# Windowed attention on one core: loading the first query block as float32 over SyncE and casting it on GpSimd

## The chip, the cores and the metric

The kernel runs on one core of one Trainium2 chip. The metric is the device time of one launch, in microseconds (us). Before the change it was 943.04 us in the median of three runs (942.97 to 943.06). On one core a single run has no second core to be compared with, so "fast" here only means that no run lay over 1.5% above the fastest of its kernel; none did.

Five engines work side by side: TensorE (PE, its weight loads PEld), VectorE (DVE), ScalarE (ACT), GpSimd (POOL) and SyncE (SP). Sixteen DMA engines move the data between HBM and the core's SBUF.

## The reference, cut to what matters

```python
B, S, D, W = 4, 4096, 1536, 64                   # float32 q, k, v
logits = einsum('bnwd,bnud->bnwu', q_w, k_w) * D ** -0.5   # windows of 64 rows
attn   = softmax(logits)
out    = einsum('bnwu,bnud->bnwd', attn, v_w)
```

Each window of 64 rows attends to itself alone. So q, k and v are each read once and the result is written once: 302 MB in and 101 MB out, with little arithmetic on each byte.

## The kernel before

A unit is 512 rows (4 slots of 128 rows), and there are 32 units. For each, q, k and v are loaded by GpSimd's transfers, which cast float32 to float16 on the way, into one of two landing buffers each. GpSimd copies a landed block to the working buffer (`q16`, `k16`, `v16`) and at once requests the block of two units later:

```python
def hand_over(x, u, dst, m, g):
    gp.wait_ge(landed[x][u % NL], 16 * (...))   # the load has landed
    gp.wait_ge(m, u)                            # the unit before is done with the working buffer
    gp.tensor_copy(out=dst..., in_=landing[x][u % NL]...).then_inc(c_l, 1)
    ...
    gp.sem_inc(g, 1)                            # TensorE may use it
    request(x, u + NL)                          # the load of two units later

for u in range(1, N):
    hand_over("q", u, q16, m_q, g_q)
    hand_over("k", u, k16, m_k, g_k)
    gp.wait_ge(m_q, u + 1)
    store(u - 1)                                # behind it in program order: the next v
    hand_over("v", u, v16, m_v, g_v)
```

TensorE transposes q and k, multiplies them, and later multiplies the weights by v. VectorE and ScalarE empty its accumulators.

The first unit has no landing buffer: its blocks go straight into the working buffers. Its first slot of q came over SyncE as float32 into an output buffer, and GpSimd cast it; the other three slots came by GpSimd's casting transfer:

```python
first = rows(qf, 0, SLOTS, SLOTS)
nc.sync.dma_start(out=outs[0][:, 0, :], in_=first[:, 0, :D]).then_inc(d_r0, 16)
nc.gpsimd.dma_start(out=q16[:, 1:, :]..., in_=first[:, 0, D:]).then_inc(d_q0, 16)
load("k", 0, k16, d_k0)
...
load("v", 0, v16, d_v0)
for u in (1, 2):
    for x in "qkv":
        request(x, u)
nc.gpsimd.wait_ge(d_r0, 16)
nc.gpsimd.tensor_copy(out=q16[:, 0, :], in_=outs[0][:, 0, :]).then_inc(c_q, 1)
...
sy.wait_ge(c_q, 1)                       # SyncE releases TensorE
sy.sem_inc(g_q, 1)._wait_ge(d_q0, 16)
```

The softmax here doesn't subtract the row's maximum and nothing guards it: scores larger than these inputs give would overflow.

## Time and profile before

| | before |
|---|---|
| time, median | 943.04 us |
| span in the profile | 940.6 us |
| busiest engine | TensorE, 70% |
| DMA engines | full in all 40 slices |
| first transpose | 12.86 us |
| one load (3.146 MB read) or one store (3.146 MB) | 7.3 us |

How to read this: the row that is full names the bound, and the time of one transfer is then the ruler.

### The profile page before, as it was taken

The numbers are of one execution on the slowest core, as the hardware profiler recorded it, in microseconds if no ns is written. First come the engines' busy times: TensorE is split into PE (matmuls) and PEld (weight loads), VectorE is DVE, ScalarE is ACT, GpSimd is POOL, SyncE is SP. The second block draws the span as 40 slices with busy tenths as digits, with TensorE's granted clock in tenths as the row PEclk, the third lists the DMA queues.
The fourth block names the chain that finished last, engine by engine and source line by source line (L and its number), as shares of the span: only waits on it lengthen the run. The fifth ranks groups of instructions, "written<-read, shape, count | busy, mean of one in ns | idle before, by whom it ended". The sixth has DMA issues, their size and how long they took to land. (4 is left out here: it accounts for less than half of the span.)

```text
span 940.6 us, 11416 instructions
## 1 busy us (share of the span) xinstructions
PE 660.8 (70%) x4096; PEld 399.9 (43%) x3456; DVE 280.0 (30%) x453; ACT 335.8 (36%) x642; POOL 337.3 (36%) x226
## 2 busy tenths in 40 slices
PE   3787677766867767767677676776867768667673
PEld 2454345533444434454444443344434355334440
DVE  1333321333313323223332233322333223332232
ACT  1444432333333333332343324333333333343332
POOL 3344333344333443333423334233343333433221
PEclk9999987888888888887887978888888887898886
DMA  9999999999999999999999999999999999999998
GB/s 206 218 217 275 257 245 280 282 282 265 236 281 282 282 273 234 275 282 282 279 234 270 282 282 281 239 262 281 283 282 246 255 281 283 281 255 246 282 299 368
DMA packets 26796, 252.17 MB, mean 268 GB/s; under 512 B 2080, under 2 KB 2080, under 8 KB 10400
## 3 DMA queue, kind: packets, MB, share of 16 engines
q0 software_dynamic: 26352, 248.13, 100.7%
q1 hardware_dynamic: 432, 3.93, 1.1%
q14 instruction: 10, 0.08, 0.0%
q8 instruction: 2, 0.03, 0.0%
HBM read 301.99 MB, written 100.66 MB: 428 GB/s over the span
## 5 line engine op out<-in xcount | busy, mean ns | idle before, releaser
L155 PE MATMUL lt<-xq,xk 128*128 128x256 f16 x1536 | 217.2, 294 | 0.0
L143 PE MATMUL tp<-ident,k 128*128 128x128 f32 x768 | 150.7, 342 | 89.5 <-PEq L209 81.2
L292 POOL COPY v<-vl 128x3072 f32<-128x3072 f32 x31 | 85.0, 2742 | 294.6 <-DMA vl<-in_v_dram 294.6
L155 PEld LDWEIGHTS lt<-xq,xk 128*128 128x128 f16 x1536 | 160.5, 105 | 33.6
L143 PEld LDWEIGHTS tp<-ident,k 128*128 128x128 f32 x768 | 116.8, 178 | 109.7 <-issue 107.0
L143 PE MATMUL tp<-ident,q 128*128 128x128 f32 x768 | 112.6, 294 | 65.4 <-DVE xq L218 34.6
L218 ACT COPY xk<-tp 128x512 f32<-128x512 f32 x96 | 59.4, 618 | 271.7 <-ACTq L209 271.7
L184 PEld LDWEIGHTS <-et 128*128 128x128 f16 x384 | 34.6, 108 | 278.4 <-issue 272.7
L218 DVE COPY xk<-tp 128x512 f32<-128x512 f32 x96 | 66.5, 692 | 237.6 <-DVEq L209 237.6
L143 PEld LDWEIGHTS tp<-ident,q 128*128 128x128 f32 x768 | 91.3, 151 | 106.3 <-issue 105.6
L292 POOL COPY q<-ql 128x3072 f32<-128x3072 f32 x31 | 85.0, 2742 | 123.6 <-DMA ql<-in_q_dram 123.6
L292 POOL COPY k<-kl 128x3072 f32<-128x3072 f32 x31 | 85.2, 2747 | 108.8 <-DMA kl<-in_k_dram 108.8
L111 PE MATMUL o<-v,et 128*128 128x512 f16 x384 | 113.1, 439 | 0.0
L260 ACT ACTIVATE et<-lt,zeros 32x128 f16<-32x128 f32 x256 | 92.0, 360 | 39.4 <-ACTq L209 36.1
L111 PE MATMUL sp<-ones,et 128*128 128x1 f16 x256 | 25.7, 169 | 113.1 <-PEq L209 110.8
L218 ACT COPY xq<-tp 128x512 f32<-128x512 f32 x96 | 59.8, 623 | 119.4 <-ACTq L209 119.4
L247 DVE TENSOR_SCALAR out<-o,rs 128x512 f32<-128x512 f32 x128 | 91.1, 747 | 32.6 <-DVEq L209 28.3
L271 ACT ACTIVATE out<-tp,rs 128x512 f32<-128x512 f32 x64 | 44.0, 687 | 136.7 <-ACTq L209 107.9
L218 DVE COPY xq<-tp 128x512 f32<-128x512 f32 x96 | 66.3, 690 | 86.6 <-DVEq L209 86.2
L111 PE MATMUL tp<-v,et 128*128 128x512 f16 x256 | 91.9, 446 | 0.0
L237 DVE RECIPROCAL rs<-sp 128x2 f32<-128x2 f32 x64 | 10.7, 167 | 261.6 <-DVEq L209 261.5
L111 PE MATMUL lt<-v,et 128*128 128x512 f16 x128 | 57.9, 452 | 0.0
(22 smaller groups left out, 221.2 us busy)
## 6 DMA issues: line engine op xcount, KB each, us to landing
out_dram<-out POOLq DMA_DIRECT2D x31, 3072.0 KB, 61.7
ql<-in_q_dram POOLq DMA_DIRECT2D x31, 1536.0 KB, 54.9
kl<-in_k_dram POOLq DMA_DIRECT2D x31, 1536.0 KB, 54.9
vl<-in_v_dram POOLq DMA_DIRECT2D x31, 1536.0 KB, 54.9
out_dram<-out SPq DMA_DIRECT2D x2, 1536.0 KB, 8.4
k<-in_k_dram POOLq DMA_DIRECT2D x1, 1536.0 KB, 17.7
v<-in_v_dram POOLq DMA_DIRECT2D x1, 1536.0 KB, 24.1
q<-in_q_dram POOLq DMA_DIRECT2D x1, 1152.0 KB, 11.1
```

The costliest lines, as they stand in the source:

```text
L111: return nc.tensor.add_instruction(mybir.InstMatmult(name=nc.get_next_instruction_name(), engine=PE, ins=[low(rhs), low(w)], outs=[low(o)] ...
L143: ins = nc.tensor.transpose(tps[g % 2][:, r, j, :], pairs[:, c * P : (c + 1) * P], ident[:, :])
L155: ins = nc.tensor.matmul(lts[h][:, r, :, :], lhsT=halves(xk, c)[:, r, h, :, w], rhs=halves(xq, c)[:, :, h, :, w], start=(c == 0 and w == 0 ...
L184: ld = nc.tensor.ldweights(w)
L218: copy(out=dst, in_=tps[g % 2][:, :, :, :]).then_inc(f_c[g % 4], 1)
L237: ve.reciprocal(out=rs[:, n : n + R], in_=sp[:, n : n + R]).then_inc(n_d, 1)
L247: ins = ve.tensor_scalar_mul(scaled(u, n, j), bank(n, j), scalar1=rs[:, n : n + 1])
L260: ins = sc.activation(ets[h][s, :, :, s], lts[h][s, :, :, s], EXP, bias=zeros[s, 0:1], scale=scale)
L271: ins = sc.activation(scaled(u, n, j), bank(n, j), COPY, bias=0.0, scale=rs[:, n : n + 1])
L292: gp.tensor_copy(out=dst[:, :, :].bitcast(FP32), in_=landing[x][u % NL][:, :, :].bitcast(FP32)).then_inc(c_l, 1)
```

## The change

Its intent is a plainer start. The first q comes whole, as float32, over SyncE in one transfer, so GpSimd has one issue less. GpSimd casts it in one instruction, which stands behind its eight load issues.

```diff
-        first = rows(qf, 0, SLOTS, SLOTS)
-        nc.sync.dma_start(out=outs[0][:, 0, :], in_=first[:, 0, :D]).then_inc(d_r0, 16)
-        nc.gpsimd.dma_start(
-            out=q16[:, 1:, :].rearrange("p r d -> p (r d)"), in_=first[:, 0, D:]
+        nc.sync.dma_start(
+            out=slots(outs[0], 0, SLOTS, SLOTS), in_=rows(qf, 0, SLOTS, SLOTS)
         ).then_inc(d_q0, 16)
         load("k", 0, k16, d_k0)
 ...
-        nc.gpsimd.wait_ge(d_r0, 16)
-        nc.gpsimd.tensor_copy(out=q16[:, 0, :], in_=outs[0][:, 0, :]).then_inc(c_q, 1)
+        nc.gpsimd.wait_ge(d_q0, 16)
+        nc.gpsimd.tensor_copy(out=q16[:, :, :], in_=outs[0][:, :, :]).then_inc(c_q, 1)
 ...
         sy.wait_ge(c_q, 1)
-        sy.sem_inc(g_q, 1)._wait_ge(d_q0, 16)
+        sy.sem_inc(g_q, 1)
```

More of the change, by code (lines that the diff above doesn't have):

```diff
@@ L72 @@
     sp = ps("sp", [P, 4])
-    d_r0, d_q0, d_k0, d_v0 = (sem(n) for n in ("d_r0", "d_q0", "d_k0", "d_v0"))
+    d_q0, d_k0, d_v0 = (sem(n) for n in ("d_q0", "d_k0", "d_v0"))
     landed = {x: [sem(f"d_{x}{i + 1}") for i in range(NL)] for x in "qkv"}
```

## The prediction

> **What bounds the kernel now.** I read the page first, for the span, the busy shares and the DMA row.
>
> ```profile
> span 940.6 us, 11416 instructions
> ...
> PE 660.8 (70%) x4096; PEld 399.9 (43%) x3456; DVE 280.0 (30%) x453; ACT 335.8 (36%) x642; POOL 337.3 (36%) x226
> ...
> DMA  9999999999999999999999999999999999999998
> ...
> HBM read 301.99 MB, written 100.66 MB: 428 GB/s over the span
> ```
>
> No engine is busy more than 70%, while the 16 DMA engines are full in all 40 slices. So the transfers bound the kernel, and the test of any change is whether it adds bytes, adds transfer time, or lets the transfer queue run empty.
>
> Next, the start in the timeline, of which I show the GpSimd (POOL) steps and the first TensorE step.
>
> ```profile
> 0.95 0.38 SPq L303 DMA_DIRECT2D out<-in_q_dram  x1
> ...
> 1.48 0.68 POOL L304 DMA_DIRECT2D q<-in_q_dram  x1 [1.04 <-SPq L300]
> ...
> 7.30 1.51 POOL L319 CAST q<-out 128x1536 f16<-128x1536 f32 x1
> 12.86 1.57 PEld L143 LDWEIGHTS tp<-ident,q 128*128 128x128 f32 x8 [12.86 <-issue]
> ...
> 34.47 2.75 POOL L292 COPY q<-ql 128x3072 f32<-128x3072 f32 x1 [25.66 <-DMA ql<-in_q_dram]
> ...
> 41.74 2.75 POOL L292 COPY k<-kl 128x3072 f32<-128x3072 f32 x1 [3.40 <-DMA kl<-in_k_dram]
> ...
> 45.59 0.72 POOL L277 DMA_DIRECT2D out_dram<-out  x1
> ...
> 49.05 2.74 POOL L292 COPY v<-vl 128x3072 f32<-128x3072 f32 x1 [2.75 <-DMA vl<-in_v_dram]
> ```
>
> Each of these copies starts when its load lands, 7.3 us after the one before, not when the unit before it has finished. One load reads 3.146 MB from HBM; 3.146 MB in 7.25 us is 434 GB/s. The other landings fit the same ruler, from the list of DMA issues (last number: microseconds from issue to landing):
>
> ```profile
> out_dram<-out POOLq DMA_DIRECT2D x31, 3072.0 KB, 61.7
> ql<-in_q_dram POOLq DMA_DIRECT2D x31, 1536.0 KB, 54.9
> ...
> k<-in_k_dram POOLq DMA_DIRECT2D x1, 1536.0 KB, 17.7
> v<-in_v_dram POOLq DMA_DIRECT2D x1, 1536.0 KB, 24.1
> q<-in_q_dram POOLq DMA_DIRECT2D x1, 1152.0 KB, 11.1
> ```
>
> Added to their issue times: the rest of q0 (the first q) lands at 12.6, k0 at 2.16 + 17.7 = 19.9, v0 at 3.03 + 24.1 = 27.1. A steady load lands some 55 us after its issue, so seven transfers of 7.3 us stand in the queue: it does not live from hand to mouth. From k0's landing at 19.9 to the last v's copy at 917.4 there are 1 + 93 loads and 29 stores: 897.5 / 123 = 7.30 us each, and three more stores (21.9 us) give 939.3, next to the span of 940.6. That is the whole span, explained by transfers alone.
>
> **What the Trainium skill says.** "DMA: Bandwidth & Descriptors", Anatomy of one DMA, gives some 2 us fixed plus bytes over 436 GB/s; the trace agrees (434 GB/s, and slot 0 of q0, 0.79 MB, took 6.3 us beside other traffic). The same page, Issuing engines are not separate DMA queues, says that transfers from SyncE and GpSimd run on the same 16 engines and interleave, and its section Queues, rings and completion order says that an engine takes its queues in turn. The window table agrees as far as it goes: between 3 and 5 us, with both queues open, it shows 403 and 321 GB/s of written bytes, between the 217 of casting loads alone and the 434 of an uncast one. "GPSIMD Engine Reference", Engine selection, calls one-input elementwise work there about line rate; the trace has 1.51 us for 1536 columns, 0.98 ns each.
>
> **The change, part by part.**
>
> *Bytes.* HBM bytes stay: q0 is 3.146 MB read, as before. Only what is written into SBUF grows: three slots of float32 for float16, from 1.18 to 2.36 MB. Loads that write half (217 GB/s written, 434 read) and stores that write all (3.146 MB) both take 7.3 us, so a transfer costs by its larger side, and this growth should cost nothing: q0 stays a 7.25 us job.
>
> *Issues.* One GpSimd issue of 0.68 us goes; the eight left come 0.7 us earlier. The SyncE transfer still goes out at 0.95 us, so the engines start moving at the same time (in windows of 1 us, the DMA share is 0.17 in the second and 0.75 in the third microsecond).
>
> *Landing of q0.* Alone, from about 2.2 us: 7.25 of transfer and 2 of completion make 11.4. Sharing evenly with k0 all along, 2.2 + 14.5 + 2 = 18.7. SyncE's queue has a start of about 1.5 us before GpSimd's first bytes, so I estimate 17.5 us, and k0 no later than its 19.9, since both together are the same two jobs.
>
> *Cast.* 6144 columns for 1536: 4 x 1.51 = 6.0 us, all of it now on the path to the first transpose; before, the small cast ended at 8.8 while the other slots landed at 12.6. The first transpose starts at 17.5 + 6.0 + 0.3 (the gap from landing to TensorE before: 12.6 to 12.9) = 23.8 us instead of 12.9: **11 us later**.
>
> *What of it survives.* Unit 0 waited for k0 before (transposes of q ended at 18.8, those of k began at 20.16); that 1.4 us goes, so k's transposes begin at 29.7 instead of 20.16, 9.5 us later. Now each thing that unit 0 releases, against the landing that it has to beat:
> - q16 free (last copy of q, 19.6 before): about 30 after. q1 lands at 34.5. Hidden.
> - k16 free (last copy of k begins at 28.3 before): about 38. k1 lands at 41.7. Hidden, 4 us to spare.
> - v16 free (end of unit 0's outputs, 37.8 before): about 47.5. v1 lands at 49.05. Hidden by 1.5 us, or late by one or two.
> - The first store (45.59 before) waits on GpSimd for unit 1's last q copy, which follows unit 0's last product: about 52. The v1 copy stands behind it in program order, and begins at about 53 instead of 49; its new load goes out at about 56 instead of 52.4.
>
> So GpSimd slips by some 6 us and then 4. At 52 us the queue still holds q2, k2, v2, q3 and k3, which land from 56.4 to 86.1: more than 30 us of work. The order in the queue is program order and does not change, so a store or load put in 6 us late starts where it would have. TensorE's unit needs about 23 us when nothing is late (37.5 to 60 or so for unit 1), a unit's transfers 3 x 7.3 us until the first store gets its turn and 4 x 7.3 = 29.2 after that. So the lag shrinks from unit 2 on, and v3, which lands at 100.7 after store 0, should find GpSimd waiting. Nothing of the 11 us reaches the end. The sum: 943.0 + 0 (path) + 0 (bytes) + some tenths either way from how the two queues mix in the first 17 us.
>
> **The rivals.**
>
> *The late start goes through.* If units ran back to back, the end would move by the full 9 to 11 us: about 953, still only 1.1% slower. Against it: GpSimd's waits in the first 120 us are all for landings, and TensorE has 30% idle to catch up with. I give it 4%.
>
> *The queue runs dry for a moment.* GpSimd being late by 6 us with stores and loads costs if the queue were shorter than that. It would give 944 to 949. Against it: some 55 us from issue to landing. Some 5%.
>
> *The bytes written count.* If a float32 write cost beyond the read, 1.18 MB / 434 GB/s = 2.7 us: 945.7. The stores, at the same 7.3 us, speak against it. Some 8%.
>
> *A gain at the start.* From 5 to 10 us the page's windows show 205 GB/s written where steady loads show 217: about 5% lost in 5 us while small and large transfers from two queues mix. One large uncast transfer may move better: up to 1 us faster, 942. Some 15%.
>
> **Range and chances.** Most weight is on no change, within what the three runs before show (942.97 to 943.06) and a spread of a few tenths of a per cent for another run: 943.2 us, 8 in 10 from 941.5 to 945.3. None of the rivals reaches 2% (18.9 us) either way; what is left there is something unseen, such as a transfer from SyncE that holds up GpSimd's queue. Faster 0.01, within 2% 0.97, slower 0.02.
>
> **What would show it.** Right: the q0 landing 14 to 19 us; one cast of 5.9 to 6.2 us; first transpose between 20 and 26; k0, v0 and q1 landing within 1 us of 19.9, 27.1 and 34.5; the first store issued at about 52; GpSimd waiting for DMA again from unit 3 on, with the v3 copy within 1 us of 100.7; the DMA row full throughout; the last v copy within 2 us of 917.4. Wrong: landings from k1 on shifted by the same amount right to the end (the bytes or the mixing count), a DMA slice below 9 between 60 and 120 us (the queue ran dry), or v copies that wait for their buffer and not for DMA past unit 4 (TensorE does not catch up).

## The result, and the profile after

The changed kernel took 942.58 us in the median of six runs (942.19 to 943.18), the kernel before 942.93 us (942.65 to 943.06) over its six. The ratio is 0.9997 with a 95% interval of 0.9984 to 1.001: the same time. Ratios here are the mean time of one kernel's fast runs over that of the other's of the same rounds, so not quite the ratio of the medians quoted.

The page of the changed kernel, in the lines that answer to those shown of before:

```profile
span 940.6 us, 11415 instructions
...
PE 656.9 (70%) x4096; PEld 397.2 (42%) x3456; DVE 279.9 (30%) x453; ACT 335.6 (36%) x642; POOL 341.0 (36%) x225
...
DMA  9999999999999999999999999999999999999998
...
HBM read 301.99 MB, written 100.66 MB: 428 GB/s over the span
```

Same span, same bytes of HBM, same full DMA row. The start itself has changed a good deal. The timeline of the changed kernel (start, duration, engine, line; in brackets the idle time before and what ended it):

```profile
0.96 0.38 SPq L302 DMA_DIRECT2D out<-in_q_dram  x1
...
17.80 5.30 POOL L317 CAST q<-out 128x6144 f16<-128x6144 f32 x1 [10.99 <-DMA out<-in_q_dram]
23.47 1.57 PEld L143 LDWEIGHTS tp<-ident,q 128*128 128x128 f32 x8 [23.47 <-issue]
...
34.17 2.75 POOL L292 COPY q<-ql 128x3072 f32<-128x3072 f32 x1 [11.07 <-DMA ql<-in_q_dram]
...
41.42 2.75 POOL L292 COPY k<-kl 128x3072 f32<-128x3072 f32 x1 [3.37 <-DMA kl<-in_k_dram]
...
50.01 0.72 POOL L277 DMA_DIRECT2D out_dram<-out  x1 [4.73 <-ACTq L216]
...
50.73 2.76 POOL L292 COPY v<-vl 128x3072 f32<-128x3072 f32 x1
```

The first transpose comes 10.6 us later (23.47 against 12.86). Yet q1 and k1 are copied when they land, 0.3 us earlier than before. Of these steps only the first store (50.01 against 45.59) and the first v copy (50.73 against 49.05) are late, and they no longer wait for a transfer. What becomes of that lateness is in GpSimd's timeline of the changed kernel, two units on:

```profile
90.83 0.71 POOL L277 DMA_DIRECT2D out_dram<-out  x1 [0.73 <-ACTq L216]
100.77 2.74 POOL L292 COPY v<-vl 128x3072 f32<-128x3072 f32 x1 [9.22 <-DMA vl<-in_v_dram]
...
119.62 0.71 POOL L277 DMA_DIRECT2D out_dram<-out  x1
```

The third store waits 0.73 us for ScalarE, the fourth not at all, and the v copy at 100.77 waits 9.22 us for its landing. In the kernel before, the same copy stands at 100.72. The lag is gone after three units, and the last v copy starts at 917.38 in both kernels.

The list of transfers of the changed kernel (KB written, us from issue to landing):

```profile
ql<-in_q_dram POOLq DMA_DIRECT2D x31, 1536.0 KB, 54.9
...
out<-in_q_dram SPq DMA_DIRECT2D x1, 3072.0 KB, 16.8
...
k<-in_k_dram POOLq DMA_DIRECT2D x1, 1536.0 KB, 18.0
```

The first q lands at 0.96 + 16.8 = 17.8 us, and k0, issued at 1.48, at 19.5. The two share the engines and land almost together. A steady load still lands 54.9 us after its issue: the queue is as deep as before.

### The profile page after: what moved, and what is told of

Same layout as the page of the kernel before. It is cut to its first block, busy times and chain, and to the rows that moved or that the text cites. A ratio compares the mean times of both kernels' runs of the same rounds, so it can differ in the third digit from the quotient of the medians.

```text
span 940.6 us, 11415 instructions
## 1 busy us (share of the span) xinstructions
PE 656.9 (70%) x4096; PEld 397.2 (42%) x3456; DVE 279.9 (30%) x453; ACT 335.6 (36%) x642; POOL 341.0 (36%) x225
## 5 line engine op out<-in xcount | busy, mean ns | idle before, releaser
L143 PE MATMUL tp<-ident,k 128*128 128x128 f32 x768 | 146.9, 335 | 82.9 <-PEq L209 71.7
L143 PEld LDWEIGHTS tp<-ident,k 128*128 128x128 f32 x768 | 113.9, 174 | 102.8 <-issue 100.2
L237 DVE RECIPROCAL rs<-sp 128x2 f32<-128x2 f32 x64 | 10.7, 168 | 259.5 <-DVEq L209 259.3
## 6 DMA issues: line engine op xcount, KB each, us to landing
ql<-in_q_dram POOLq DMA_DIRECT2D x31, 1536.0 KB, 54.9
kl<-in_k_dram POOLq DMA_DIRECT2D x31, 1536.0 KB, 54.9
vl<-in_v_dram POOLq DMA_DIRECT2D x31, 1536.0 KB, 54.9
out<-in_q_dram SPq DMA_DIRECT2D x1, 3072.0 KB, 16.8
```

The lines of the kernel that those rows point to most:

```text
L143: ins = nc.tensor.transpose(tps[g % 2][:, r, j, :], pairs[:, c * P : (c + 1) * P], ident[:, :])
L237: ve.reciprocal(out=rs[:, n : n + R], in_=sp[:, n : n + R]).then_inc(n_d, 1)
```

## The experiments

My theory: the transfers bound the kernel, and the nine transfers put out at the start let compute begin late at no cost as long as that queue does not run dry. The rival: compute's start counts in full or in part. A second question is whether float32 in place of float16 in SBUF costs transfer time, and a third what a standstill of the engines costs. Every edit below is to the changed kernel, whose 942.58 us is the base; each run was timed in three rounds beside the kernel before (942.8 to 943.1 us), and all gave correct results.

### e1: the cast shared by three engines

```diff
-        nc.gpsimd.tensor_copy(out=q16[:, :, :], in_=outs[0][:, :, :]).then_inc(c_q, 1)
+        nc.gpsimd.tensor_copy(out=q16[:, 0, :], in_=outs[0][:, 0, :]).then_inc(c_q, 1)
+        nc.vector.wait_ge(d_q0, 16)
+        nc.vector.tensor_copy(out=q16[:, 1:3, :], in_=outs[0][:, 1:3, :]).then_inc(c_q, 1)
+        nc.scalar.wait_ge(d_q0, 16)
+        nc.scalar.copy(out=q16[:, 3, :], in_=outs[0][:, 3, :]).then_inc(c_q, 1)
 ...
-        sy.wait_ge(c_q, 1)
+        sy.wait_ge(c_q, 3)
```

> The cast is shared out: VectorE two slots, ScalarE one, GpSimd one, all behind the same landing at 17.8 us. First transpose at about 20.5 us instead of 23.5. My theory (transfers bound the kernel, the start of compute is hidden by the queue): 942.6 us, within 1 us of the changed kernel. Rival (the start of compute counts): 939.5 us, 3 us faster.

Measured: 942.61 us (942.33 to 942.97), with the first transpose at 20.86. Compute starts 2.6 us earlier and the time stays. The theory holds, and the cast is not worth speeding up here.

### e2, e3, e4: the cast seven, nine and thirteen times

```diff
-        nc.gpsimd.tensor_copy(out=q16[:, :, :], in_=outs[0][:, :, :]).then_inc(c_q, 1)
+        for i in range(7):          # 9 and 13 in e3 and e4
+            nc.gpsimd.tensor_copy(out=q16[:, :, :], in_=outs[0][:, :, :]).then_inc(c_q, 1)
+            nc.gpsimd.wait_ge(c_q, i + 1)
 ...
-        sy.wait_ge(c_q, 1)
+        sy.wait_ge(c_q, 7)          # 9 and 13
```

> The cast of 5.3 us runs seven times instead of once, one after the other: 6 x 5.3 = 31.8 us more before the first transpose, which comes at about 55.3 us. My theory: the nine transfers issued up front keep the DMA engines busy until v2 has landed at 70.7 us; the first of the next issues (q3) would follow unit 0's last q copy at 62, so at about 65.5 us, just in time. 943 us, at most 946. Rival (a late start goes through to the end): 942.6 + 31.8 = 974 us.

> The cast runs nine times: 8 x 5.3 = 42.4 us more, first transpose at about 66 us. My theory: q3 is issued at about 76 us, but the engines run out at about 69 us; the queue is dry for 9 us or so, and for one or two more around the first store: 954 us (950 to 958), and the DMA row of the profile shows a slice well below 9. Rival (goes through): 985 us. Rival (hidden without limit): 942.6 us.

> The cast runs thirteen times: 12 x 5.3 = 63.6 us more. My theory: beyond the point where the queue runs dry each further microsecond counts in full, so this is e3_cast_x9 plus 4 x 5.3 = 21.2 us, about 975 us. Rival (goes through from the first microsecond): 1006 us. A slope well below 1 between e3 and e4 would say that the queue refills and hides part of it again.

| | first transpose | time, median |
|---|---|---|
| e1 | 20.9 us | 942.61 us |
| changed kernel | 23.5 us | 942.58 us |
| e2 | 55.5 us | 944.78 us |
| e3 | 66.4 us | 956.24 us |
| e4 | 87.5 us | 976.98 us |

This is a flat line with a knee. The first 32 us of delay (23.5 to 55.5) cost 2.2 us; from e3 to e4, 21.1 us of delay cost 20.7 us. The knee lies where the queue runs dry. The page's DMA row of e3:

```profile
DMA  9987999999999999999999999999999999999997
```

And windows of 2 us of e3 around that place (busy time of PE, PEld, DVE, ACT and POOL with the number of instructions, then clock, DMA share and GB/s written):

```profile
66.00:68.00 2.00, 1.60 (x8) 1.57 (x8) 0.36 (x1) 0.00 (x0) 0.01 (x1) 1.00 1.02 212
68.00:70.00 2.00, 1.87 (x10) 1.51 (x8) 0.62 (x2) 0.63 (x1) 0.00 (x0) 1.00 0.31 61
70.00:72.00 2.00, 1.79 (x10) 1.12 (x9) 0.80 (x2) 0.62 (x1) 0.00 (x0) 1.00 0.00 0
...
76.00:78.00 2.00, 2.00 (x21) 1.77 (x19) 0.49 (x1) 0.62 (x1) 0.08 (x1) 1.00 0.73 98
...
92.00:94.00 2.00, 1.36 (x11) 0.88 (x9) 1.08 (x2) 0.66 (x1) 1.30 (x2) 1.00 0.43 98
```

The engines stop between 68 and 70 us, where the nine transfers end, and start again after q3's issue at 75.53; a second, shorter dip follows at the first store (issued at 92.70), as expected. The expected issue times (76 us for q3 in e3, 65.5 in e2) were right within 0.5 us, and the knee lies where they put it: e2's q3 is just in time, e3's is not.

e2 lies inside its expected range but 2.2 us above the changed kernel. This lateness is there in full at the v copy of unit 6 (2.2 us) and stays to the last (2.3), so it is not the slow loss described under e7. Its DMA share falls to 0.88 in the 2 us behind the first store's issue at 82.01 and to 0.69 from 112 to 114 us; but the changed kernel, too, has a 0.83 at its first store (82 to 84 us). What the 2.2 us are made of stays open.

### e5, e6: one more transfer, as float32 or with the cast in it

```diff
+        # e5: SyncE, behind its first transfer
+        nc.sync.dma_start(out=slots(outs[1], 0, SLOTS, SLOTS),
+                          in_=rows(qf, UR, SLOTS, SLOTS)).then_inc(d_x0, 16)
+        # e6 instead: GpSimd, behind v0
+        nc.gpsimd.dma_start(out=outs[1][:, 0:2, :]....bitcast(FP16),
+                            in_=rows(qf, UR, SLOTS, SLOTS)[:, 0, :]).then_inc(d_x0, 16)
+        # both: waited for before v0 is released to TensorE
+        sy.wait_ge(d_x0, 16)
```

> SyncE loads a second float32 block of 3.146 MB (the rows of q1, into an output buffer that unit 1 overwrites) right after the first; it holds up only the release of v0 to TensorE. My theory (a transfer costs by its larger side, and its time adds to the end): 942.6 + 7.25 = 949.9 us. Rival (what comes early lies in the head beside compute that has not begun, so it is hidden): 942.6 us.

> As e5, but GpSimd issues the extra load with the cast in the transfer: 3.146 MB read, 1.573 MB written, behind v0 in its queue. My theory (reads set the time of a load): the same 7.25 us more, 949.9 us, within 0.5 us of e5. Rival (bytes written into SBUF count): half, 946.2 us. That also prices the growth from float16 to float32 in the change: 0 against about 2.7 us.

Measured: e5 950.15 us (949.86 to 950.5), e6 949.95 us (949.74 to 950.16). So 7.6 and 7.4 us more than the changed kernel, and within 0.2 us of each other. The landing of q1, from GpSimd's timeline of e5:

```profile
41.42 2.75 POOL L292 COPY q<-ql 128x3072 f32<-128x3072 f32 x1 [18.39 <-DMA ql<-in_q_dram]
```

and of e6:

```profile
41.48 2.75 POOL L292 COPY q<-ql 128x3072 f32<-128x3072 f32 x1 [18.32 <-DMA ql<-in_q_dram]
```

Against 34.17 that is 7.25 and 7.31 us, whether 3.146 or 1.573 MB were written (the two also differ in the queue, SyncE's or GpSimd's). Both read the same, so between these two loads the bytes written made no difference. And the time counts although the compute engines have hardly begun: 7.3 us more of transfers in the head cost 7.4 to 7.6 us at the end, while 32 us more of cast in the same head cost 2.2.

### e7: GpSimd waits for the first q before its first issue

```diff
+        nc.gpsimd.wait_ge(d_q0, 16)
         load("k", 0, k16, d_k0)
 ...
-        nc.gpsimd.wait_ge(d_q0, 16)
         nc.gpsimd.tensor_copy(out=q16[:, :, :], in_=outs[0][:, :, :]).then_inc(c_q, 1)
```

> GpSimd waits for q0 before its first load issue instead of behind the eighth. The first q has all 16 engines to itself and lands at about 11.5 us instead of 17.8; eight issues of 5.3 us and the cast of 5.3 us then put the first transpose near 22 us, almost where it is in the changed kernel. My theory: what counts is the time in which the engines stand still between q0's last byte and k0's first, 2 to 3.5 us: 944.6 to 946 us. Rival (the start of TensorE is what counts): 941 to 942.6 us.

Measured: 948.45 us (947.67 to 949.16), 5.9 us more, with the first transpose at 23.59, 0.1 us from where it is in the changed kernel. So the same start of compute gives another time, and a time in the direction of the standing engines, but more than I had expected. The windows of 1 us of e7, same columns as above:

```profile
10.00:11.00 1.00, 0.00 (x0) 0.00 (x0) 0.00 (x0) 0.00 (x0) 0.00 (x0) 1.00 0.19 57
11.00:12.00 1.00, 0.00 (x0) 0.00 (x0) 0.00 (x0) 0.00 (x0) 0.00 (x0) 1.00 0.00 0
12.00:13.00 1.00, 0.00 (x0) 0.00 (x0) 0.00 (x0) 0.00 (x0) 0.45 (x1) 1.00 0.00 0
13.00:14.00 1.00, 0.00 (x0) 0.00 (x0) 0.00 (x0) 0.00 (x0) 0.91 (x3) 1.00 0.33 37
```

From the shares, the standstill is 0.81 + 1 + 1 + 0.67 = 3.5 us, and q1's copy starts at 37.66 against 34.17, also 3.5. The last v copy starts at 924.02 against 917.38: 6.6 us. So about half of this delay is the standstill, at the upper end of what I expected, and the other half comes afterwards, in small steps of the landings between units 3 and 20, with the DMA row full (more on it under e10). The theory is right in kind, and it left out this second part.

### e8: the first q by GpSimd's casting transfer like all others

```diff
-        nc.sync.dma_start(
-            out=slots(outs[0], 0, SLOTS, SLOTS), in_=rows(qf, 0, SLOTS, SLOTS)
-        ).then_inc(d_q0, 16)
+        load("q", 0, q16, d_q0)
         load("k", 0, k16, d_k0)
 ...
-        nc.gpsimd.wait_ge(d_q0, 16)
-        nc.gpsimd.tensor_copy(out=q16[:, :, :], in_=outs[0][:, :, :]).then_inc(c_q, 1)
 ...
-        sy.wait_ge(c_q, 1)
-        sy.sem_inc(g_q, 1)
+        sy.sem_inc(g_q, 1)._wait_ge(d_q0, 16)
```

> The first q comes as one casting load through GpSimd's queue like all others: no SyncE load, no cast, no mixing of two queues. First transpose at 11 to 13 us. My theory: the engines start moving at about 2.7 us instead of about 1.9, and all else is the same transfers in one queue: 943.0 to 943.6 us. Rival (mixing two queues costs transfer time): about 941.5 us. Rival (an earlier start of compute pays): 932 us.

Measured: 944.02 us (943.82 to 945.42), ratio to the kernel before 1.0014 (0.9997 to 1.0031), so not told apart from it by that interval. The first transpose comes at 12.41, 11 us earlier than in the changed kernel, and buys nothing: both rivals named in the expectation fall. The median lies 0.4 us above my own 943.6, though. q1's copy began at 34.01, not later than in the changed kernel, and the lateness appears afterwards, as in e7 (the last v copy is 1.8 us later than in the changed kernel). The later start of the engines that I expected is there all the same: in the second and third microsecond the DMA share is 0.00 and 0.74 against 0.41 and 1.13, which makes 0.8 us. Why q1's landing does not show it is said under e10.

### e9, e10: does the loss after a standstill follow from its length, or from how the queues restart?

```diff
+        # e9: the wait and the cast before the first issue
+        nc.gpsimd.wait_ge(d_q0, 16)
+        nc.gpsimd.tensor_copy(out=q16[:, :, :], in_=outs[0][:, :, :]).then_inc(c_q, 1)
         load("k", 0, k16, d_k0)
 ...
-        nc.gpsimd.wait_ge(d_q0, 16)
-        nc.gpsimd.tensor_copy(out=q16[:, :, :], in_=outs[0][:, :, :]).then_inc(c_q, 1)
```

```diff
+        # e10: three slots first, then the fourth together with GpSimd's loads
+        nc.sync.dma_start(out=outs[0][:, 0:3, :]..., in_=first[:, 0, : 3 * D]).then_inc(d_x0, 16)
+        nc.sync.wait_ge(d_x0, 16)
+        nc.sync.dma_start(out=outs[0][:, 3, :], in_=first[:, 0, 3 * D :]).then_inc(d_q0, 16)
+        nc.gpsimd.wait_ge(d_x0, 16)
         load("k", 0, k16, d_k0)
```

> e7 cost 5.9 us where its engines stood still for about 3.5; the landings show 3.0 us of delay at unit 2 and 6.6 from unit 19 on, so half was lost slowly after the restart. Here GpSimd also does its cast before the first issue: the standstill grows by the cast, 5.3 us, and TensorE starts earlier, near 18 us. Theory A (a restart of the queue costs some 3 us extra once, whatever the gap's length): 948.5 + 5.3 = 953.8 us. Theory B (the cost grows with the gap, 5.9 for 3.5): 942.6 + 1.7 x 8.8 = 957.5 us. Rival (an earlier start of TensorE pays): below 948 us.

> The same bytes and the same standstill as e7, but the restart is mixed: three slots of the first q come first, both engines wait for them, then SyncE's last slot and GpSimd's loads start together. Theory C (the slow loss follows only when all engines restart in step on one queue; in the changed kernel they start on two): about 3.3 us of standstill and no drift afterwards, 945.5 to 946.5 us. If the drift follows any restart: 948 to 949 us, with the v copies' delay growing from about 3 to over 6 us between units 2 and 19.

Measured: e9 953.09 us (952.72 to 953.86), e10 948.37 us (948.16 to 948.57). How much later than in the changed kernel GpSimd's copies start, in us:

| | copy of q1 | v copy of unit 3 | of unit 20 | of unit 31 | time against 942.58 |
|---|---|---|---|---|---|
| e7 | 3.5 | 4.0 | 6.6 | 6.6 | +5.9 |
| e9 | 8.4 | 8.1 | 9.8 | 9.8 | +10.5 |
| e10 | 2.8 | 3.3 | 6.2 | 6.2 | +5.8 |
| e8 | -0.2 | -0.5 | 1.1 | 1.8 | +1.4 |
| e5 | 7.3 | 7.0 | 7.5 | 7.5 | +7.6 |

e9 speaks against theory B (a cost that grows 1.7 times as fast as the gap: 957.5): 4.9 us more standstill at q1 cost 4.6 us more time. TensorE began at 18.90 there, 4.6 us earlier than in the changed kernel, and the kernel was 10.5 us slower. Theory A's 953.8 is close, but its one fixed extra is not fixed: 1.4 us are lost after q1 in e9 and 3.1 in e7. Theory C falls: e10 restarts on two queues at once and drifts as e7 does, by 3.4 us. The loss is not one of compute, since in e7 and e10 all q, k and v copies wait for landings.

The kept traces tell more. A transfer reports its end in 16 counts on its semaphore, and it has landed with the last of them; the packed trace holds the time of each, though not which of the 16 DMA engines sent it. In us:

| | first to last count, q1 | the same, last v | mean of the 16 counts later than in the changed kernel, q1 | the same, last v |
|---|---|---|---|---|
| changed kernel | 2.1 | 2.5 | | |
| e7 | 0.6 | 4.5 | 4.65 | 4.75 |
| e9 | 0.8 | 2.7 | 9.45 | 9.67 |
| e10 | 0.6 | 4.5 | 3.99 | 4.15 |
| e8 | 0.8 | 3.2 | 0.85 | 0.91 |
| e5 | 1.8 | 2.8 | 7.48 | 7.25 |

In the mean next to nothing is lost after q1. The whole cost is there from the start, 4.65 us in e7, and the 3.5 us read above are only what the last count shows of it; e9's longer standstill adds 4.8 us in the mean for 4.9 at q1's copy. What grows afterwards is the distance between the first and the last count. After a late or interrupted start the 16 counts begin close together (0.6 to 0.8 us) and move apart to 2.7 to 4.5 us, and each landing waits for the last. Why they move apart, and further in e7 and e10 than in e9, stays open.

No experiment points to a version that beats both kernels: those that only start compute earlier (e1, e8) leave the time where it is or lengthen it a little, and those that add a transfer or hold transfers back (e5 to e7, e9, e10) lengthen it.

## Why the prediction was right

The number alone shows little, since no change was forecast; the path has to be checked step by step. Two of the signs named in advance failed: the cast took 5.30 us (5.9 to 6.2 was said), and the first store went out 2 us earlier than said. By unit 3 nothing is left of either.

**The bound.** Right. A full DMA row and landings 7.3 us apart carried the whole argument. e5 and e6 confirm it from the other side: one transfer more, one ruler's length more at the end.

**Bytes.** Right. e6 against e5 prices half the written bytes at 0.2 us within the noise, so the third rival ("the bytes written count", 2.7 us) falls.

**Landing of q0.** 17.8 us for 17.5. With all engines to itself the same transfer lands at 0.96 + 11.3 = 12.3 us (e7), so sharing with k0 cost it 5.5 us. The prediction's "the trace agrees" holds for the rate alone: no line that it shows measures the 2 us of completion.

**Cast.** 5.30 us for 6.0. I scaled the small cast of 1.51 us by four; at 5.30 us for 6144 columns the cost is 0.86 ns a column, not 0.98. A part that does not grow with the columns would explain it (0.25 us, an estimate from these two casts), but no run tests that.

**First transpose.** 23.47 us for 23.8: the later landing took back about half of what the shorter cast saved.

**What survives of the 10.6 us.** Right in kind, and too pessimistic by 2 us: the first store went out at 50.01 for "about 52", the v1 copy at 50.73 for "about 53", its new load at 54.1 for "about 56". The step that was mis-sized is the length of unit 0: from the first transpose to the first product with v it took 18.7 us before (12.86 to 31.53), and 16.0 after (23.47 to 39.48). I had taken off the 1.4 us of waiting for k0, of which 1.0 came (7.3 us from the first transpose of q to the first of k before, 6.2 after). The other 1.6 us lie in the stretch from the first transpose of k to the first product with v: 11.4 us before, 9.8 after, with TensorE busy for 10.1 and 8.7 us on the same number of recorded matmuls (72). Its granted clock there was 0.85 in the mean before, with 0.50 from 22 to 25 us, and 1.00 after. In e2, e3, e7 and e10 it was 1.00 as well, and the stretch took 9.8 us in each; in e8 and e9, at 0.84 and 0.85, it took 10.9 and 10.7. (e1 took 10.2 us at 1.00, so the clock is not all.) I had carried over a stretch that ran at a lowered clock. The lag was gone by unit 3, as said: v3's copy at 100.77 for 100.7.

**The late-start rival.** It falls with e1 and e8, where compute starts 3 and 11 us earlier and gains nothing, and with e2, where it starts 32 us later and loses 2.2.

**The dry-queue rival.** It is real but far away. e2 to e4 place the knee at 53 to 55 us for the first transpose, some 30 us beyond the changed kernel (53 is where the line through e3 and e4 meets 942.58).

**The gain at the start.** Half seen, and oversized: 5% of 5 us, the prediction's own figures, is 0.3 us and not 1. q1 landed 0.3 us earlier than before, but at unit 3 the two kernels were level again, and the last v copies start at the same 917.38. The time differs by 0.3 us, inside the interval; nothing is shown there.

## What to carry to other kernels

Before working on a kernel's start, look whether the DMA row is full and how long the transfers already issued last. Here the nine issued at the start last until about 70 us, and compute could begin some 30 us later at next to no cost, because the next issue still came in time. That is less than the 55 us from issue to landing: e3's delay of 43 us cost 13.7. Starting compute earlier was worth nothing. Anything that added a transfer, or kept the first loads from being issued, cost its full length or more. In such a kernel judge an edit of the start by the landing of the first steady load and not by when the first matmul runs; and compare a late landing too, since in e7, e8 and e10 the last of the landings was 2 to 3.4 us later still.

## What the Trainium skill lacked or had wrong

- A casting load's price: in "DMA: Bandwidth & Descriptors" I found no word on which side sets it. Here 3.146 MB read cost 7.25 us when all of it was written and 7.31 us when half was (e5, e6).
- The same page's 2 us plus bytes over 436 GB/s, which it gives for GpSimd's transfers, would make an estimate of 9.2 us for the first float32 q; from SyncE, with the engines to itself, it took 11.3 us from issue to landing, and k0, issued by GpSimd to engines that stood still, took 10.5 (e7).
- No page that I read says how far apart the 16 end counts of one transfer lie, or that they move apart after a late or interrupted start: from 0.6 us at q1 to 4.5 at the last v in e7 and e10, and from 0.8 to 2.7 in e9. The last landing was later for it by 3.1, 3.4 and 1.4 us than the delay at q1.
